# In-projection of a two-layer step: one ordered list of loads, two more tile buffers, and TensorE in written order

## Chip, cores, metric

One core of a Trainium2 chip. The metric is the device time of one execution in microseconds (us); the time of a kernel is the median of its runs.

## What is computed

One inference step of a two-layer backbone with D = 2048, for 128 context tokens and 128 latent tokens (256 columns in all). The change lies at the very start, in the first layer's modulated norm and its combined input projection:

```
mod = silu(cond) @ w_ada[0] + b_ada[0]                 # cond: two rows, (2, 2048) @ (2048, 6*2048)
sh1, sc1, gt1, sh2, sc2, gt2 = split(mod, 6)
h = rmsnorm(x, g_norm_mix[0]) * (1 + sc1) + sh1        # x: (256, 2048)
proj = h @ w_in_ab[0]                                  # (2048, 2880): queries, latents, keys, values
...                                                    # attention, out-projection, ConvFFN, second layer
```

Everything is float32. `w_ada[0]` is needed for sc1 and sh1 before any row of h exists; each is 2048 x 2048.

## The kernel before

Activations lie transposed: 16 chunks of 128 features on the partitions, 256 token columns (`x[:, c]`). A float32 product is made of three fast ones: each operand is split into a rounded high half and the rest (`hx` holds both halves of h; `wh`, `wl` those of a weight block), and `gemm` issues high x high, high x low, low x high for every 128 x 128 block. `split` does the halves: ScalarE casts the high one (L238), VectorE subtracts for the low one (L239). `Weights` loads tiles of 8 or 16 blocks into the buffers `raw` (three of 1 MB) and splits them when `chunk` runs out of blocks.

The in-projection (`mixer_ab`, `part`) runs over k in pieces, because h becomes ready piece by piece: chunks 0 and 1 against all 23 output columns, then chunks 2 and 3, then three times four chunks (quarters 2, 3 and 4). Each column's product goes to a PSUM tile `acc` (three of them) and is copied to (first piece) or added to (the others, VectorE, L957) the projection held in SBUF: `proj`, `kvb`, `qb`.

The adaLN vectors come from TensorE too: `condw` holds the two conditioning rows as a narrow stationary operand, and a *unit* (layer, vector j, quarter q) is four 1 MB tiles of `w_ada`, 16 matmuls in four column groups of one PSUM bank `ada` (`sum_rows`, L525 loads), a copy `am` to SBUF, four transposes, a reduction to `mod` and, for scales, one more step to `scl` (`ada_finish`). The first quarter of scale (j = 1) and shift (j = 0) is done in *half units* (`load_half`, `half_unit`, L358 and L368 to L378) of two tiles each, because only chunks 0 and 1 are needed to start. The adaLN tiles go to `araw` (two buffers); for the first eight units every second tile goes to one of the three `raw` buffers instead.

Before the first product the kernel loads all constants (`cst`), x in four pieces, the four tiles of two half units and a weight tile; takes the mean square of x (ScalarE squares, VectorE adds; `stat_rstd`, `norm_scale`); and makes the rows of chunks 0 and 1 with `modulate`: x times the norm factor (L597), scale and shift (L603 on VectorE, L606 on ScalarE), high half (L607), low half (L592, on VectorE and GpSimd by turns). Later rows are made by `modulate` once both units of their quarter are finished; `pump` and `ensure` spread the adaLN steps over the columns at set rates (`RATE`).

Order: a scheduler orders the instructions of each engine by a simulated time line, except for those passed to `keep_order`, which stay behind the instruction traced before them on their engine. `pe.in_turn` does this for all of TensorE's matmuls; before the change it is on in quarters 2 and 3 only. A load waits at the head of its queue (SP) until the buffer that it overwrites has been read.

Of the kernel before, what the change touches and what calls it, by code (L numbers as in the profile page):

```python
# [38 lines left out]
    ("ident", 128), ("ones", 128), ("pick", 32), ("inv", 5), ("mhalf", 16),  # L39
    ("rch", 128), ("rsh", 128), ("rcm", 128), ("rsm", 128),  # L40
    ("cond", 32), ("bada", NL * 6 * KD),
    ("gmix", NL * KD), ("gffn", NL * KD), ("gfin", 16),
# [8 lines left out]
NCONST = _n  # L51
RATE = {"in0": 0.35, "in": 0.5, "in3": 0.25, "heads": 0.72, "out0": 0.62, "c": 0.36, "outc": 0.36}
# [37 lines left out]
def step_kernel(ctx: ExitStack, tc: tile.TileContext, A: dict):  # L90
# [54 lines left out]
    sp.dma_start(out=cst, in_=A["cst"])  # L145
# [18 lines left out]
    act.activation(condw[:, :, 0:2], C("cond").rearrange("p (k r) -> p k r", r=2), AF.Silu)  # L164

# [49 lines left out]
    def bank():  # L215
        return T_(pmisc, [P, 512], "misc")
# [26 lines left out]
    class Weights:  # L243
# [9 lines left out]
        def load(self):  # L253
            raw = T_(wpool, [P, 4, 512], "raw").rearrange("p g n -> p (g n)")
            sp.dma_start(out=raw, in_=self.src[self.at])
            self.at += 1
            return raw

        def ahead(self, pin):

            if not self.half:
                self.half = [self.load(), 0]
            raw, lo = self.half
            self.blocks += self.halves(raw, lo, pin)
            self.half = None if lo else [raw, 8]

        def halves(self, raw, lo, pin=lambda i: i):
            wh = T_(wpool, [P, 1024], "wh", F32R, bufs=4)
            wl = T_(wpool, [P, 1024], "wl", F32R, bufs=4)
            for at in range(0, 8, FINE):  # L270
                s = slice(at * P, (at + FINE) * P)
                split(wh[:, s], wl[:, s], raw[:, (lo + at) * P:(lo + at + FINE) * P], pin)
            return [(wh[:, b * P:(b + 1) * P], wl[:, b * P:(b + 1) * P]) for b in range(8)]

        def chunk(self):
            while len(self.blocks) < self.nblk:
# [3 lines left out]
                n = self.per  # L280
                if self.cycle:
                    n = min(n, self.cycle - self.at * n % (-(-self.cycle // n) * n))
                n *= self.nblk if self.per < TB else 1
                raw = T_(wpool, [P, 4, 512], "raw").rearrange("p g n -> p (g n)")
                sp.dma_start(out=raw[:, :n * P], in_=self.src[self.at, :, :n * P])
                self.at += 1
                n0 = FINE if fine[0] else 8
                for lo in range(0, n, n0):
# [8 lines left out]
                    for b in range(hi - lo):  # L297
                        s = slice(b * P, (b + 1) * P)
                        self.blocks.append((wh[:, s], wl[:, s]))
            out, self.blocks = self.blocks[:self.nblk], self.blocks[self.nblk:]  # L300
            return out

    def first_three(W, xh, xl, order, mid=None, fixed=False):
# [3 lines left out]
        raws = [W.load() for _ in range(3)]  # L307
# [39 lines left out]
    ada = {"i": 2, "t": 0, "due": 0.0, "pew": 1.0}  # L347
# [6 lines left out]
    def load_half(j, h, tag):  # L354

        raws = [T_(wpool, [P, 4, 512], tag, **({"bufs": 2} if tag == "araw" else {})) for _ in range(2)]
        for t, raw in enumerate(raws):
            sp.dma_start(out=raw, in_=A["w_ada"][0, j, 0, 2 * h + t])  # L358
        return [raw.rearrange("p g n -> p (g n)").rearrange("p (b n) -> p b n", b=8) for raw in raws]

    def half_unit(j, h, raws, pin=lambda i: i):
        ps = T_(ppool["ada"], [P, 512], "ada", bufs=1)
        for k in range(KD):
            g = k % 4
            pin(pe.matmul(ps[32 * g:32 * g + 32, :NT], condw[:, k, :], raws[k // 8][:, k % 8],
                          start=(k < 4), stop=(k >= KD - 4), skip_group_check=True))
        am = T_(tmp, [P, 512], "am", bufs=1)
        act.copy(am[:, :NT], ps[:, :NT])  # L368
        pt = T_(ppool["ada"], [P, 512], "ada", bufs=1)
        for b in range(2):  # L370
            pe.transpose(pt[:, b * P:(b + 1) * P], am[:, b * P:(b + 1) * P], ident)
        at = slice(2 * h, 2 * h + 2)
        out = mod[:, 0, j, at]
        dve.tensor_reduce(out=out, in_=pt[:, :NT].rearrange("p (b g r) -> p b r g", b=2, g=4)[:, :, 0:2],
                          axis=AX.X, op=ALU.add)
        dve.tensor_tensor(out=out, in0=out, in1=vector("bada", 0, j, 0)[:, at], op=ALU.add)
        if j == 1:
            dve.scalar_tensor_tensor(out=scl[:, 0, 0, at], in0=out, scalar=1.0,  # L378
                                     in1=vector("gmix", 0, 0, 0)[:, at], op0=ALU.add, op1=ALU.mult)
        if h == 1:  # L380
            done.add((0, j, 0))
# [129 lines left out]

    def row_step(until=len(ROWS)):
# [68 lines left out]
    def norm_scale(st):  # L581
        return spread(stat_rstd(st, D))

    def modulate(hx, rb, l, which, chunks, fixed=False):
# [26 lines left out]
        for c, h in lows:  # L611
            low(c, h)

# [920 lines left out]
```

## Time and profile before

| | us |
|---|---|
| median of 3 runs | 2322.47 |
| lowest, highest | 2320.69, 2327.41 |
| profiled execution | 2323.0 |
| its span | 2321.2 |
| first product of the in-projection starts | 29.02 |
| first product on chunks 2 and 3 | 54.25 |
| quarter 2, quarter 3, quarter 4 start, about | 83, 128, 174 |

The profile shows one execution on the engines TensorE (PE, with its weight loads PEld), VectorE (DVE), ScalarE (ACT), GpSimd (POOL) and the load queue of SyncE (SP). Times in a row of the timeline are start and length; `xN` is a count; an arrow in brackets names what ended an idle stretch. A busy PE is not PE at its peak, since pipelined matmuls overlap in the records; start-to-start times are used for its rates.

### The profile page before, as it was taken

Reading aid. Unit: us, or ns where it says so; the run is one execution under the profiler, and the core shown is the slowest. Engines: PE = TensorE matmul, PEld = TensorE weight load, DVE = VectorE, ACT = ScalarE, POOL = GpSimd, SP = SyncE. Lnnn points to the kernel's source line nnn. Section 1 sums busy time; section 2 is a strip of 40 time slices with the busy share of each in tenths; the row PEclk is TensorE's granted clock in tenths of the full one; section 3 lists DMA queues with packets and bytes.
Section 4 is the critical chain, followed back from the end, with each engine's and each line's share of the span. In section 5 each row is a group of like instructions: output and inputs, shape, how many; then the busy total and the mean of one; then the engine's idle time right before and its main releaser. Section 6 shows DMA issues by size and latency. Waiting matters only on the chain.

```text
span 2321.2 us, 47505 instructions
## 1 busy us (share of the span) xinstructions
PE 2279.7 (98%) x19478; PEld 2183.0 (94%) x19478; DVE 1885.4 (81%) x2955; ACT 1202.8 (52%) x1982; POOL 197.7 (9%) x242
## 2 busy tenths in 40 slices
PE   6999999999999999999999999999999999999998
PEld 5778868999999999999999999999999999999998
DVE  4568978989999999999988979898999965666654
ACT  4246555575554355555575455457655434555543
POOL 0002211210000000000140001024000000000011
PEclk9999999999999999999999999999999999999999
DMA  9997888777777877777787888766767655555553
GB/s 373 338 345 271 327 312 307 288 287 262 261 265 280 307 266 255 260 266 258 281 323 279 299 324 303 294 258 221 255 251 272 254 200 200 191 191 199 192 192 127
DMA packets 99834, 617.15 MB, mean 266 GB/s; under 512 B 10720, under 2 KB 18720, under 8 KB 32928
## 3 DMA queue, kind: packets, MB, share of 16 engines
q1 hardware_dynamic: 99616, 614.11, 71.7%
q8 instruction: 153, 2.51, 0.4%
q14 instruction: 65, 0.53, 0.1%
HBM read 609.32 MB, written 4.75 MB: 265 GB/s over the span
## 4 chain that ended last, share of the span: by engine, by line
PE 83%; DMA 1%; DVE 0%; ACT 0%; POOL 0%; issue 0%; DVEq 0%; ACTq 0%
PE acc L105 80%; PE ada L105 1%; PE att L105 1%; DMA araw<-w_ada 1%; PE att L108 0%; DVE x L1396 0%; PE ada L108 0%; DVE wl L239 0%; PE misc L105 0%; ACT wh L238 0%; POOL rr L212 0%; DVE hx L239 0%; ACT hx L238 0%; ACT p L799 0%; PE misc L108 0%
## 5 line engine op out<-in xcount | busy, mean ns | idle before, releaser
L105 PE MATMUL acc<-hx,wh 128*128 128x256 f32 (+1 forms) x7264 | 1257.9, 278 | 4.4 <-ACT hx L607 1.4
L238 ACT CAST wh<-raw 128x1024 fp32r<-128x1024 f32 (+2 forms) x826 | 795.1, 974 | 881.2 <-PE acc L105 709.0
L105 PEld LDWEIGHTS acc<-hx,wh 128*128 128x128 f32 x7264 | 1098.8, 188 | 33.9 <-issue 14.7
L239 DVE TENSOR_TENSOR wl<-raw,wh 128x1024 fp32r<-128x1024 f32 (+2 forms) x826 | 923.0, 1133 | 247.8 <-ACT wh L238 242.9
L105 PE MATMUL acc<-hx,wl 128*128 128x256 f32 (+1 forms) x3632 | 1006.5, 278 | 5.3 <-DVE wl L239 5.3
L105 PEld LDWEIGHTS acc<-hx,wl 128*128 128x128 f32 x3632 | 683.7, 188 | 9.3 <-DVE wl L239 7.2
L105 PE MATMUL acc<-g,wh 128*128 128x256 f32 x2816 | 478.8, 276 | 0.0
L105 PEld LDWEIGHTS acc<-g,wh 128*128 128x128 f32 x2816 | 423.6, 188 | 0.0
L105 PE MATMUL acc<-g,wl 128*128 128x256 f32 x1408 | 388.0, 276 | 0.0
L433 DVE CUSTOM_DVE_ANT_0 junk<-araw,condb 128x2048 f32<-128x2048 f32 x128 | 294.2, 2298 | 0.0
L105 PE MATMUL acc<-hxc,wh 128*128 128x256 f32 (+1 forms) x1568 | 282.9, 282 | 0.0
L105 PEld LDWEIGHTS acc<-g,wl 128*128 128x128 f32 x1408 | 264.1, 188 | 0.0
L105 PEld LDWEIGHTS acc<-hxc,wh 128*128 128x128 f32 x1568 | 241.5, 189 | 4.6 <-issue 4.2
L105 PE MATMUL acc<-hxc,wl 128*128 128x256 f32 (+1 forms) x784 | 218.5, 279 | 0.0
L201 POOL TENSOR_TENSOR sqacc<-sqacc,sq 128x256 f32<-128x256 f32 x62 | 74.0, 1193 | 1499.3 <-ACT sq L197 1499.1
L105 PEld LDWEIGHTS acc<-hxc,wl 128*128 128x128 f32 x784 | 147.5, 188 | 0.4
L1288 ACT ACTIVATE cv<-acc,convw 128x256 f32<-128x256 f32 x169 | 94.4, 559 | 0.0
L105 PE MATMUL ada<-araw,condw 128*32 128x512 f32 (+1 forms) x640 | 78.6, 587 | 14.3 <-ACT sq L197 13.3
L485 DVE CUSTOM_DVE_ANT_0 hx<-block,condb 128x1024 fp32r<-128x1024 f32 x65 | 79.2, 1219 | 7.5 <-DMA block<-w_ada 5.4
L1294 DVE SCALAR_TENSOR_TENSOR cv<-acc,convw,cv 128x254 f32<-128x254 f32 x169 | 80.9, 479 | 3.2
L767 DVE SCALAR_TENSOR_TENSOR x<-acc,mod,x 128x128 f32<-128x128 f32 x190 | 57.2, 342 | 30.3 <-PE acc L105 30.3
L1291 DVE SCALAR_TENSOR_TENSOR cv<-acc,convw,cv 128x254 f32<-128x254 f32 x169 | 80.2, 475 | 0.0
(241 smaller groups left out, 1538.3 us busy)
## 6 DMA issues: line engine op xcount, KB each, us to landing
raw<-w_up SPq DMA_DIRECT2D x176, 1024.0 KB, 4.8
araw<-w_ada SPq DMA_DIRECT2D x138, 1024.0 KB, 5.7
raw<-w_down SPq DMA_DIRECT2D x88, 1024.0 KB, 4.8
raw<-w_in_c SPq DMA_DIRECT2D x48, 1024.0 KB, 6.5
block<-w_ada SPq DMA_DIRECT2D x41, 512.0 KB, 6.4
raw<-w_in_ab SPq DMA_DIRECT2D x19, 1024.0 KB, 7.2
raw<-w_out_ab SPq DMA_DIRECT2D x16, 1024.0 KB, 7.0
raw<-w_out_c SPq DMA_DIRECT2D x16, 1024.0 KB, 7.1
```

The lines of the kernel that those rows point to most:

```text
L105: return self.placed(nc.tensor.matmul(*a, **kw))
L201: eng.tensor_tensor(out=st["acc"], in0=st["acc"], in1=sq, op=ALU.add)
L238: pin(act.copy(out_hi, src))
L239: pin(dve.tensor_tensor(out=out_lo, in0=src, in1=out_hi.bitcast(F32), op=ALU.subtract))
L433: keep_order(dve.tensor_tensor_reduce(out=T_(feat["pool"], [P, D], "junk"), in1=feat["row"][:, c], in0=feat["raw"].rearrange("p g n -> p ( ...
L485: keep_order(dve.tensor_tensor_reduce(out=self.junk, in0=self.raw, in1=self.row[:, c].rearrange("p (g n) -> p g n", g=2), scale=1.0, scala ...
L767: dve.scalar_tensor_tensor(out=x[:, c, s], in0=ps[:, s], scalar=mod[:, l, 3 * which + 2, c, g:g + 1], in1=x[:, c, s], op0=ALU.mult, op1=AL ...
L1288: pin(act.activation(y, ps, AF.Identity, scale=cw[:, 1, m:m + 1], bias=cw[:, 3, m:m + 1]))
L1291: pin(dve.scalar_tensor_tensor(out=y3[:, :, 1:], in0=p3[:, :, :T - 1], scalar=cw[:, 0, m:m + 1], in1=y3[:, :, 1:], op0=ALU.mult, op1=ALU.add))
L1294: pin(dve.scalar_tensor_tensor(out=y3[:, :, :T - 1], in0=p3[:, :, 1:], scalar=cw[:, 2, m:m + 1], in1=y3[:, :, :T - 1], op0=ALU.mult, op1=A ...
```

## The change

Loads of the in-projection's first four pieces are put into one list, `feed`, in order of need: an entry is issued when a buffer of its kind is free, and an entry that has none holds all behind it. Buffers are counted by hand: three for weights, two `araw`, and two more of 1 MB, `s1` and `s3`, which lie where `ql` and `kv_in` will be later. Tiles 1 and 3 of a unit use these; weights have the three `raw` buffers to themselves.

TensorE's order is written out: `pe.in_turn` is on from the first half unit to the end of quarter 3, and dictionaries by column (`first_half`, `other_half`, `quarter`) say after which column a pair of adaLN tiles is summed (`pair`), a unit turned (`turned`) or rows begun. The matmuls of two tiles of a unit stand together.

The rows of chunks 0 to 7 are made in two steps: `scaled_rows` (norm factor and scale, before the shift is there) and `begin_row` (shift with the rounding to the high half on ScalarE, low half on VectorE). Quarters 3 and 4 still use `modulate`, now after column 19 instead of 18.

At the start: only the first 373 columns of constants are loaded ahead of x; the rest (`late_constants`) come in the list. The squares of x are taken in four pieces of four chunks. Nine idle matmuls on a zero tile (`WARM`) are issued first. The first weight tile is loaded in two halves, and its first half is split ahead of the first rows. The two half units no longer share a PSUM bank.

Quarter 4 and all later stages keep their code; the layout of the constants is reordered. The diff, cut:

```
+NEARLY = _AT["bada"][0] + 2 * KD
+WARM = 9
...
-    sp.dma_start(out=cst, in_=A["cst"])
+    keep_order(sp.dma_start(out=cst[:, :NEARLY], in_=A["cst"][:, :NEARLY]))
...
+            w = n * P // parts
+            for i in range(parts):
+                s = slice(i * w, (i + 1) * w)
+                pin(sp.dma_start(out=raw[:, s], in_=self.src[self.at, :, s]))
...
+    class Feed:
+        def __init__(self):
+            self.items, self.tiles = [], {}
+            self.free = {"a": 2, "s1": 1, "s3": 1, "raw": 3, "late": 1}
+        def add(self, home, load, key=None):
+            self.items.append((home, load, key))
+        def go(self):
+            while self.items and self.free[self.items[0][0]]:
+                home, load, key = self.items.pop(0)
+                self.free[home] -= 1
+                self.tiles[key] = load()
+        def use(self, home):
+            self.free[home] += 1
+            self.go()
...
-            if ada["i"] < 8 and t % 2:
-                ada["raw"] = T_(wpool, [P, 4, 512], "raw")
-            else:
-                ada["raw"] = T_(wpool, [P, 4, 512], "araw", bufs=2)
+            ada["raw"] = T_(wpool, [P, 4, 512], "araw", bufs=2)
...
+    def scaled_rows(rb, c0, n):
+        for c in range(c0, c0 + n):
+            h = T_(tmp, [P, NT], "nt", bufs=4)
+            keep_order(dve.tensor_tensor(out=h, in0=x[:, c], in1=rb, op=ALU.mult))
+            for g in range(2):
...
+                keep_order(dve.tensor_scalar(out=h[:, s], in0=h[:, s], scalar1=scl[:, 0, 0, c, g:g + 1],
+                                             scalar2=None, op0=ALU.mult))
...
+    def begin_row(hx, h, c):
+        for g in range(2):
...
+            keep_order(act.activation(hx[:, c, s], h[:, s], AF.Identity, bias=b_))
+            keep_order(dve.scalar_tensor_tensor(
+                out=hx[:, c, NT + g * T:NT + (g + 1) * T], in0=h[:, s], scalar=b_,
+                in1=hx[:, c, s].bitcast(F32), op0=ALU.add, op1=ALU.subtract))
...
+                half_load(1, 0)
+                half_load(0, 0)
+                weights(whole, 2)
+                half_load(1, 1)
+                weights(whole)
+                half_load(0, 1)
+                feed.add("late", late_constants)
+                weights(whole)
+                units(2, (0, 1))
+                weights(halves)
+                units(2, (2, 3))
+                weights(halves)
+                units(3, (0, 1, 2, 3))
+                weights(halves)
+                weights(rest)
+                for q in (1, 2):
+                    for u, ts in ((2 * q + 2, (0, 1)), (2 * q + 2, (2, 3)), (2 * q + 3, (0, 1)), (2 * q + 3, (2, 3))):
+                        weights(rest)
+                        units(u, ts)
+                    weights(rest)
+                    weights(rest)
+                feed.go()
+
+                pe.in_turn = True
...
+                whole.ahead(keep_order, first_rows)
...
+                first_half = {0: lambda: whole.ahead(keep_order), 4: lambda: half_begin(1), 6: lambda: half_end(1),
+                              10: lambda: stretch(2, 2), 13: lambda: half_begin(0), 15: lambda: half_end(0),
+                              22: lambda: pair(2, 0)}
+                other_half = {5: lambda: pair(2, 2), 7: turned, 10: lambda: stretch(4, 4), 12: lambda: pair(3, 0),
+                              15: lambda: pair(3, 2), 17: four_rows, 20: split_next, 22: split_next}
+                def quarter(q):
+                    u = 2 * q + 2
+                    return {4: lambda: pair(u, 0), 8: lambda: pair(u, 2), 10: turned, 13: lambda: pair(u + 1, 0),
+                            17: lambda: pair(u + 1, 2), 19: lambda: turned(q + 1)}
...
+                part(whole, 0, 2, True, 0, at(first_half))
+                part(halves, 2, 2, False, 0, at(other_half))
+                for q in (1, 2):
+                    part(rest, 4 * q, 4, False, 0, at(quarter(q)))
+                pe.in_turn = False
...
+        for _ in range(WARM):
+            keep_order(pe.matmul(ps, idle[:, :P], idle, start=True, stop=True))
```

More of the change, by code (lines that the diff above doesn't have):

```diff
@@ L164, in step_kernel @@
     act.activation(condw[:, :, 0:2], C("cond").rearrange("p (k r) -> p k r", r=2), AF.Silu)
+    warm = T_(small, [P, 2], "rv")
+    keep_order(act.activation(warm, condw[:, 0, 2:4], AF.Silu))
     def load_cw(l):
@@ L256, in load, with begin, take @@
             self.at += 1
-            return raw
-        def ahead(self, pin):
-            if not self.half:
[L262 to L267, printed above, removed]
+            return raw, n
+        def begin(self, parts=1):
+            self.begun.append(self.load(parts, keep_order))
+        def take(self):
+            return self.begun.pop(0) if self.begun else self.load()
@@ L268, in halves, with ahead @@
+        def ahead(self, pin, mid=None):
+            if not self.half:
+                self.half = [*self.take(), 0]
+            raw, n, lo = self.half
+            self.blocks += self.halves(raw, lo, pin, mid, min(8, n - lo))
+            self.half = None if lo else [raw, n, 8]
+            if lo:
+                self.used()
+        def halves(self, raw, lo, pin=lambda i: i, mid=None, n=8):
             wh = T_(wpool, [P, 1024], "wh", F32R, bufs=4)
             wl = T_(wpool, [P, 1024], "wl", F32R, bufs=4)
-            for at in range(0, 8, FINE):
-                s = slice(at * P, (at + FINE) * P)
-                split(wh[:, s], wl[:, s], raw[:, (lo + at) * P:(lo + at + FINE) * P], pin)
@@ L279, in chunk @@
                     continue
[L280 to L286, printed above, removed]
+                raw, n = self.take()
                 n0 = FINE if fine[0] else 8
@@ L352, in step_kernel @@
     later = []
[L354 to L381, printed above, removed]
```

235 lines of the change are left out of this document (175 added, 60 removed).

## The prediction

> **What bounds the kernel now.** I read the page first, then the busy time by stage, the waits of TensorE and of the load queue, and last the order of time. Bounds of the stages come from the timeline; columns are busy us (xcount) by engine, granted clock, DMA share, GB/s.
>
> ```profile
> span 2321.2 us, 47505 instructions
> PE 2279.7 (98%) x19478; PEld 2183.0 (94%) x19478; DVE 1885.4 (81%) x2955; ACT 1202.8 (52%) x1982; POOL 197.7 (9%) x242
> PE   6999999999999999999999999999999999999998
> ```
>
> ```profile
> 0.00:29.00 29.00, 12.33 (x96) 6.30 (x96) 10.71 (x31) 11.67 (x28) 1.41 (x6) 1.00 0.95 385
> 29.00:54.25 25.25, 24.54 (x207) 20.04 (x207) 10.75 (x21) 15.16 (x36) 1.96 (x2) 0.93 0.92 352
> 54.25:83.08 28.83, 25.82 (x198) 19.89 (x195) 18.02 (x43) 9.40 (x16) 2.02 (x2) 0.94 0.97 375
> 83.08:127.80 44.72, 43.21 (x349) 34.60 (x349) 26.17 (x50) 15.30 (x22) 1.63 (x2) 1.00 0.89 325
> 127.80:174.00 46.20, 43.46 (x353) 34.92 (x352) 26.82 (x50) 15.43 (x23) 1.45 (x2) 1.00 0.90 344
> ```
>
> TensorE is busy in every slice but the first, so a microsecond taken from its path in the in-projection should reach the end. The five rows are: before the first product; part A (chunks 0 and 1, with the first pair of adaLN tiles of the second quarter's shift-and-scale units); part B (chunks 2 and 3); quarter 2; quarter 3. Quarter 4 starts at about 174. No engine but TensorE is near its full time in any row, and the DMA is below its best rate in the last four.
>
> ```profile
> 126.78 0.39 PE L105 MATMUL acc<-hx,wh 128*128 128x256 f32 x2
> 127.12 0.39 PE L105 MATMUL acc<-hx,wh 128*128 128x256 f32 x2
> 86.03 1.07 PE L105 MATMUL ada<-araw,condw 128*32 128x512 f32 x8
> 87.02 0.50 PE L105 MATMUL acc<-hx,wh 128*128 128x256 f32 x2
> 26.57 1.07 PE L105 MATMUL ada<-araw,condw 128*32 128x256 f32 x16 [0.27 <-DVE mod L374]
> 101.29 0.60 PE L108 MATMUL ada<-cst,am 128*128 128x128 f32 x4
> ```
>
> These are TensorE's prices. Three products take 0.34 us from start to start (126.78 to 127.12): 0.1133 each. A 1 MB adaLN tile takes 0.99 (86.03 to 87.02), so a unit of four 4.0; a tile of the first quarter takes 1.07, a half unit of two 2.1; turning a unit takes about 0.5 of the quoted 0.60. Work of the stages at these prices: part A 138 products = 15.6, two half units 4.3, their turns 0.8, two tiles 2.0: 22.7 of 25.25. Part B 15.6, six tiles 5.9, two turns 1.0: 22.5 of 28.83. Quarters 2 and 3 each 276 products = 31.3, two units 8.0, two turns 1.0: 40.3 of 44.72 and 46.20. So 2.5, 6.3, 4.4 and 5.9 us lie between work, and 29 us before it.
>
> ```profile
> 13.34 1.94 PE L105 MATMUL ada<-araw,condw 128*32 128x256 f32 x16 [13.34 <-ACT sq L197]
> 21.68 3.64 PE L105 MATMUL ada<-raw,condw 128*32 128x256 f32 x32 [1.17 <-DVE mod L374]
> 29.02 1.60 PE L105 MATMUL acc<-hx,wh 128*128 128x256 f32 x4 [1.37 <-ACT hx L607]
> 28.00:32.00 4.00, 2.98 (x12) 2.68 (x13) 2.82 (x6) 1.27 (x4) 1.22 (x1) 0.62 1.00 411
> 72.00:76.00 4.00, 2.19 (x18) 1.19 (x10) 1.91 (x7) 3.31 (x6) 0.00 (x0) 1.00 0.95 320
> 76.00:80.00 4.00, 3.25 (x15) 3.25 (x16) 3.89 (x8) 3.61 (x8) 2.02 (x2) 0.59 1.02 401
> 108.23 0.50 PE L105 MATMUL acc<-hx,wh 128*128 128x256 f32 x2
> 109.49 0.39 PE L105 MATMUL acc<-hx,wl 128*128 128x256 f32 x1 [0.76 <-DVE wl L239]
> 173.59 0.74 PE L105 MATMUL acc<-hx,wh 128*128 128x256 f32 x4 [0.86 <-ACT wh L238]
> ```
>
> ```profile
> SPq L525 <- PE ada L105: 42.5, 19, 4.0
> ```
>
> Three kinds of loss are visible. The shift's half unit starts only at 21.68, since both half units share one PSUM bank, and it runs at half clock (32 in 3.64, against 16 in 1.07). The second quarter's rows wait for their unit in part B: TensorE is half idle at 72 to 76 and then gets a clock of 0.59. In the quarters a product waits for the low half of a weight tile that landed late (109.49, 173.59), because the load queue had waited for buffers: in the first 230 us it waited 42.5 for adaLN sums alone.
>
> **The change, part by part.**
>
> ```profile
> 8.00:12.00 4.00, 0.00 (x0) 0.00 (x0) 3.09 (x8) 2.99 (x8) 0.00 (x0) 1.00 1.04 430
> 16.00:20.00 4.00, 4.00 (x27) 2.71 (x27) 0.16 (x1) 0.37 (x1) 0.70 (x1) 1.00 1.02 426
> cst<-cst SPq DMA_DIRECT2D x1, 698.5 KB, 4.0
> x<-xT SPq DMA_DIRECT2D x4, 512.0 KB, 7.0
> araw<-w_ada SPq DMA_DIRECT2D x24, 1024.0 KB, 7.3
> 8.26 0.72 ACT L197 ACTIVATE sq<-x 128x256 f32<-128x256 f32 x2 [0.38 <-DMA x<-xT]
> ```
>
> *Landing times.* The queue runs at about 424 GB/s while nothing blocks it. The constants and the first adaLN tile are 3.86 MB, 9.1 us at this rate, and are used at 13.34; constants and two pieces of x are 1.76 MB, 4.2 us, used at 8.26. So a tile lands about 4.1 us after the list's bytes over 0.424. The new list starts with 373 of the constants' columns (0.19 MB), x 2.10, and four tiles 4.19: 6.48 MB, landed at 19.4; the first half of the first weight tile follows at 20.6.
>
> ```profile
> 25.44 0.37 ACT L368 COPY am<-ada 128x256 f32<-128x256 f32 x1 [6.07 <-PE ada L105]
> 27.79 0.88 ACT L606 ACTIVATE nt<-nt,mod,scl 128x128 f32<-128x128 f32 x2
> L239 DVE TENSOR_TENSOR wl<-raw,wh 128x1024 fp32r<-128x1024 f32 x31 | 37.2, 1220 | 15.2 <-ACT wh L238 15.1
> L238 ACT CAST wh<-raw 128x1024 fp32r<-128x1024 f32 x32 | 32.2, 1050 | 57.1 <-DMA raw<-w_in_ab 51.5 <-DVE proj L957 5.6
> L957 DVE TENSOR_TENSOR proj<-proj,acc 128x256 f32<-128x256 f32 x33 | 13.6, 419 | 27.2 <-PE acc L105 27.2
> L603 DVE TENSOR_SCALAR nt<-nt,scl,mod 128x128 f32<-128x128 f32 x16 | 4.5, 342 | 0.1
> L105 PE MATMUL misc<-cst,rr 128*128 128x128 f32 x4 | 1.2, 462 | 0.0
> ```
>
> *The front.* Last tile 19.4, its sums 1.07 to 20.5; ScalarE first casts the weight half (pinned ahead, landed 20.6, about 0.55) and then copies the sums, 0.4, to 21.6; two transposes and two small VectorE steps bring the shift by 22.8; one row's two activations 0.9 more. First product at about 24.0 instead of 29.0: 5.0 gained. The nine idle products (nine of two passes) are unpriced: four passes over 128 columns took 1.2, so 512 columns are about 1 us a pass cold, half of that warm; 9 to 18 us from about 1. Below 12 they are hidden, since the first tile lands at 12.0; above, they delay only the scale's half unit, which has until 19.4. I take no cost; at the far bound the first product is some 3 us later.
>
> The clock: in the row 28 to 32 it fell to 0.62 although no idle stretch just before exceeded 1.37. TensorE will again be mostly idle from 20.5 to 24, so I charge the same half-clock stretch once more, 1.7 us. [...]
>
> *Part A*: 22.7 of work, 1.7 of clock, 0.6 of small gaps: 24.0 to 49.0, against 54.25. Gain so far 5.2. Its second and third weight tiles land at 29.3 and 37.7; with 2.3 for cast and low half (the rows of L238 and L239) they are there at 31.6 and 40.0, when TensorE wants them at about 33 and 41. It fits without slack.
>
> *Part B*: the rows of the second quarter are scaled early (moved, so nothing new), and at their shift only an activation and one VectorE step per half remain; the stall at 72 to 76 and its slow clock go. Next late is the third weight tile: 26.7 MB into the list, landed 67.0, usable 69.3, needed at about 67; and VectorE has 23 adds of 0.419, 5.75 low halves of 1.22, two tiles split ahead for 2.4, four rows of about 1.1 and six of 0.7: 27 us of work in a stretch of 25, some of it started earlier. I charge 2.0. Part B ends at 49.0 + 22.5 + 2.0 = 73.5 against 83.08: gain 9.5.
>
> *Quarters 2 and 3*: with four adaLN buffers and three for weights a load no longer waits for the tile just before it. In quarter 3 a pair of buffers comes free at the fifth column; the next pair lands some 7.3 (the araw row) and 2.5 later and is used 15 us on, after nine columns of 1.36, another pair and a turn. I leave 1.5 of small gaps to each: 41.8 and 41.8, against 44.72 and 46.20: 7.3 gained, of which I keep 6.5, for the rows of the next quarter now have three columns (4 us) of cover instead of four; that cover gone, they would cost about 2.
>
> *Quarter 4 and after* keep their rates and start 16 earlier, at 158. The scheduler may order a few things otherwise; I take 0.5 off. Sum: 9.5 + 6.5 - 0.5 = 15.5 less than the profiled execution's 2323.0 (its span of 2321.2 and 1.8 around it), which is 0.5 above the median of 2322.47: 2307.
>
> **Rivals.** *The load rate* (0.15). Over a longer stretch the trace shows 375 GB/s (54 to 83), with blocked loads in it. Were that the rate itself, part B's last weight tile is usable at 77.6 and quarter 2 starts at about 83, as now; only 6.5 remain: 2316. [...]
>
> *Slower: the written order* (0.13). Before, in parts A and B, TensorE could take any ready product; now it stands at a pair of adaLN tiles until both have landed, and all weights wait behind. Twelve pairs stand there. Each late pair costs its lateness, and above some 1.4 us of idle also a slow clock, 1.7. The gain is gone at 1.3 us a pair; at 2 us it is 24 lost against 15.5 won: 2331. For it: no slack in part A, one blocked entry holds all loads behind it, and ScalarE's copy of the sums is pinned too, so that casts queue behind a late pair. Against it: from part B on, by the landing times above, pairs are early.
>
> *It does not reach the end* (0.05): a later stage bound by loads would give the time back: 2320. The page's slices after the first speak against it.
>
> **How the numbers follow.** 0.3%, about 7 us, is what a measurement here can tell from no change. The forecast has 0.67, with 9 to 23 of gain (3 from the idle products, 2 from VectorE and rows, 2 from order on the one side; the clock, the charged gaps on the other). Faster 0.67, within 0.3% 0.20 (load rate and lost gain), slower 0.13. The range reaches from 2299 over the first two rivals to 2322.
>
> **What would show it.** First product at 23 to 25 and part B's start near 49: front right. A granted clock under 0.7 after it: the clock step right. Quarter 2 starting at 72 to 76 with rates above 410 until 60: the list right; at 82 or later with the share at 1.0: the load rate. Waits of TensorE for adaLN tiles, or idle gaps ahead of pairs, totalling over 10: the written order. Quarters of 41 to 43 confirm the buffers. Wrong would be a first product after 27, or quarter 4 starting after 168.

## The result, and the profile after

| | us |
|---|---|
| before, median of 6 runs | 2325.07 (2320.69 to 2327.41) |
| changed, median of 6 runs | 2309.88 (2308.48 to 2311.19) |
| changed / before | 0.9937, 95% interval 0.9925 to 0.995 |
| changed, profiled execution and its span | 2308.48, 2306.7 |

The change makes the kernel 0.6% faster: 14.5 us between the two profiled spans, where the prediction's sum was 15.5, and both 2309.88 and 2308.48 lie within its range. The medians above differ by 15.2; in a later group of runs, where the kernel before had 2320.56, the same changed kernel was 11.7 below it, so the gain is known to a few us only. The page of the changed kernel looks as before; only the first slice has moved.

```profile
span 2306.7 us, 47528 instructions
PE   8999999999999999999999999999999999999998
```

The busy time by stage says where the gain came from. Columns as in the prediction's table; the rows are the stretch before the first product, part A, part B, quarters 2, 3 and 4, and the heads up to the first residual of the out-projection. First the changed kernel, then two rows of the kernel before, quarter 4 and the heads, which the prediction did not show.

```profile
0.00:24.30 24.30, 18.07 (x106) 8.80 (x106) 7.76 (x18) 7.82 (x13) 1.41 (x6) 0.99 0.92 355
24.30:50.90 26.60, 25.89 (x222) 21.86 (x222) 11.36 (x28) 16.98 (x40) 0.00 (x0) 0.88 0.95 390
50.90:78.50 27.60, 23.78 (x197) 18.39 (x194) 19.29 (x49) 7.96 (x16) 0.00 (x0) 1.00 1.01 414
78.50:121.40 42.90, 41.11 (x333) 34.45 (x332) 27.64 (x55) 16.33 (x22) 0.00 (x0) 0.96 0.91 367
121.40:162.80 41.40, 41.40 (x353) 35.05 (x352) 27.31 (x52) 16.83 (x25) 1.64 (x2) 1.00 0.89 350
162.80:210.00 47.20, 47.20 (x392) 42.08 (x391) 38.45 (x84) 31.00 (x65) 11.90 (x13) 1.00 0.71 265
210.00:355.80 145.80, 141.57 (x1010) 114.57 (x1012) 117.20 (x287) 78.02 (x182) 25.19 (x48) 1.00 0.85 317
```

```profile
173.80:219.90 46.10, 45.86 (x374) 40.87 (x374) 37.82 (x80) 30.14 (x61) 10.61 (x11) 1.00 0.72 260
219.90:368.90 149.00, 144.06 (x1010) 115.00 (x1013) 117.11 (x287) 78.30 (x182) 28.81 (x48) 0.99 0.83 310
```

| stage | before | predicted | measured | gain so far, predicted | measured |
|---|---|---|---|---|---|
| front | 29.0 | 24.0 | 24.3 | 5.0 | 4.7 |
| part A | 25.2 | 25.0 | 26.6 | 5.2 | 3.3 |
| part B | 28.8 | 24.5 | 27.6 | 9.5 | 4.6 |
| quarters 2 and 3 | 90.7 | 83.6 | 84.3 | 16.0 | 11.0 |
| quarter 4 | 46.1 | | 47.2 | | 9.9 |
| heads | 149.0 | | 145.8 | | 13.1 |
| all the rest | | | | 15.5 | 14.5 |

Parts A and B together gained nothing (54.2 us after, 54.1 before) where 4.5 were forecast; the heads, whose code was not touched, became 3.2 shorter. Quarter 4 of the kernel before is taken to start at 173.8, with its row above. The bound of quarter 2's start (78.5) is counted from the turn of the second quarter's shift (74.74): five columns of 0.68 and the turn.

**Front.** TensorE's timeline (start, length), then two rows of the busy time:

```profile
20.49 1.07 PE L107 MATMUL att<-kv_in,condw 128*32 128x256 f32 x16 [1.42 <-DMA kv_in<-w_ada]
22.70 0.44 PE L110 MATMUL att<-cst,am 128*128 128x128 f32 x2 [1.14 <-ACT am L390]
24.32 0.97 PE L107 MATMUL acc<-hx,wh 128*128 128x256 f32 x2 [1.19 <-ACT hx L672]
```

```profile
24.00:28.00 4.00, 3.68 (x16) 3.58 (x17) 2.81 (x7) 3.04 (x8) 0.00 (x0) 0.50 1.02 424
28.00:32.00 4.00, 4.00 (x36) 3.52 (x38) 0.40 (x1) 1.61 (x4) 0.00 (x0) 0.66 1.01 420
```

The last shift tile's sums start at 20.49, 1.1 later than the 19.4 that was counted for its landing, and the chain of copy, turn and activation behind them takes 3.8 to the first product at 24.32, where 4.6 was counted: the chain is the one that was counted, and its two errors nearly cancel. The clock then falls to 0.50 and 0.66; the longest idle stretch since 12 is the one of 1.42.

**Part B.** Here TensorE waits for weight halves. Its waits from 50.9 to 78.5 (us in total, times, longest), its timeline around the longest, and the timeline of ScalarE:

```profile
PE acc L107 <- DVE wl L246: 2.1, 3, 1.0
PE acc L107 <- ACT wh L245: 1.7, 1, 1.7
```

```profile
72.22 0.50 PE L107 MATMUL acc<-hx,wh 128*128 128x256 f32 x2 [1.71 <-ACT wh L245]
73.48 0.39 PE L107 MATMUL acc<-hx,wl 128*128 128x256 f32 x1 [0.76 <-DVE wl L246]
...
81.07 0.38 PE L107 MATMUL acc<-hx,wl 128*128 128x256 f32 x1 [1.49 <-DVE wl L246]
```

```profile
57.91 0.59 ACT L424 COPY am<-ada 128x512 f32<-128x512 f32 x1 [6.48 <-PE ada L107]
58.39 2.00 ACT L245 CAST wh<-raw 128x1024 fp32r<-128x1024 f32 x2
70.64 0.59 ACT L424 COPY am<-ada 128x512 f32<-128x512 f32 x1 [10.25 <-PE ada L107]
71.12 1.78 ACT L245 CAST wh<-raw 128x1024 fp32r<-128x1024 f32 x2
```

ScalarE stands idle for 10.25 us in front of the copy of a unit's sums, and the casts of the next weights go right behind it. This copy (L424) is not among the instructions passed to `keep_order`; the scheduler put it there. Until TensorE comes to that pair ScalarE splits no weight, and TensorE then runs out of split ones. The weight tiles were there by then: the trace has the second one of part B landed at 55.9 and the third at 68.9, and their casts start at 58.4 and 71.1, each at the end of a copy. Then VectorE is full (3.75 and 4.00 of 4), and the clock falls again, to 0.74:

```profile
76.00:80.00 4.00, 3.28 (x27) 2.90 (x25) 3.75 (x13) 4.00 (x12) 0.00 (x0) 1.00 0.99 367
80.00:84.00 4.00, 2.93 (x17) 2.93 (x18) 4.00 (x10) 2.23 (x3) 0.00 (x0) 0.74 1.02 432
```

```profile
77.96 0.41 DVE L639 TENSOR_TENSOR nt<-x,misc 128x256 f32<-128x256 f32 x1
```

The last row is one of four multiplies of the *next* quarter's rows, which the scheduler put among the low halves that quarter 2 waits for.

**Loads.** The list kept the queue going: from 44 to 76 every stretch of 4 us has 412 to 428 GB/s. The one hole in parts A and B is at 40 to 44, after 406 at 36 to 40.

```profile
40.00:44.00 4.00, 3.47 (x44) 2.51 (x36) 1.12 (x1) 2.48 (x5) 0.00 (x0) 1.00 0.65 221
```

What the buffers did shows at ScalarE, in its waits from 78 to 216 (us in total, times, longest) for weight tiles to land. Before, in the changed kernel, and in the two runs below that go without the two extra buffers (e3, f4):

```profile
ACT wh L238 <- DMA raw<-w_in_ab: 52.0, 9, 11.2
ACT wh L245 <- DMA raw<-w_in_ab: 9.1, 3, 3.8
ACT wh L245 <- DMA raw<-w_in_ab: 41.8, 8, 10.1
ACT wh L245 <- DMA raw<-w_in_ab: 37.7, 7, 6.8
```

### The profile page after: what moved, and what is told of

Same layout as the page of the kernel before. It is cut to its first block, busy times and chain, and to the rows that moved or that the text cites. A ratio compares the mean times of both kernels' runs of the same rounds, so it can differ in the third digit from the quotient of the medians.

```text
span 2306.7 us, 47528 instructions
## 1 busy us (share of the span) xinstructions
PE 2278.7 (99%) x19504; PEld 2186.1 (95%) x19504; DVE 1887.0 (82%) x2967; ACT 1202.5 (52%) x1973; POOL 188.5 (8%) x238
## 4 chain that ended last, share of the span: by engine, by line
PE 84%; DMA 0%; DVE 0%; ACT 0%; POOL 0%; issue 0%; DVEq 0%; ACTq 0%
PE acc L107 81%; PE ada L107 1%; PE att L107 1%; PE att L110 0%; DMA araw<-w_ada 0%; DVE x L1589 0%; PE ada L110 0%; PE misc L107 0%; DVE wl L246 0%; ACT wh L245 0%; POOL rr L219 0%; DVE hx L246 0%; ACT hx L245 0%; ACT p L862 0%; PE misc L110 0%
## 5 line engine op out<-in xcount | busy, mean ns | idle before, releaser
L107 PE MATMUL ada<-araw,condw 128*32 128x512 f32 (+1 forms) x608 | 73.8, 578 | 1.3 <-DMA araw<-w_ada 1.3
```

The lines of the kernel that those rows point to most:

```text
L107: return self.placed(nc.tensor.matmul(*a, **kw))
```

## The experiments

All were timed in five rounds beside the kernel before. Landmarks compare profiled executions: the first pair of adaLN sums in quarter 2 (changed kernel 89.47), the first in quarter 3 (130.53), and the first copy of the heads (209.97, before 219.91).

| kernel | median us | ratio to before (95%) | quarter 2 pair | quarter 3 pair | heads |
|---|---|---|---|---|---|
| changed, again (a0_again) | 2308.84 | 0.9943 (0.993 to 0.9955) | 88.73 | 129.65 | 209.09 |
| e1_no_idle | 2312.91 | 0.9959 (0.9946 to 0.9971) | 92.18 | 133.46 | 212.77 |
| e2_free_order | 2313.69 | 0.9966 (0.9954 to 0.9979) | 90.63 | 135.09 | 216.70 |
| e3_no_extra_buffers | 2317.17 | 0.9979 (0.9971 to 0.9988) | 89.79 | 135.02 | 217.74 |
| e4_rows_late | 2311.32 | 0.9954 (0.994 to 0.9967) | 89.60 | 130.90 | 212.00 |
| e5_weights_first | 2310.54 | 0.9952 (0.9939 to 0.9964) | 89.61 | 130.52 | 211.24 |
| e6_cast_ahead | 2308.71 | 0.9943 (0.9931 to 0.9955) | 87.98 | 129.08 | 210.55 |
| e7_keep_clock | 2312.00 | 0.9956 (0.9942 to 0.997) | 93.25 | 134.27 | 213.71 |
| f1_multiply_later | 2310.47 | 0.9941 (0.9927 to 0.9955) | 88.26 | 130.88 | 212.27 |
| f2_cast_and_multiply | 2308.09 | 0.9932 (0.9919 to 0.9944) | 86.02 | 128.64 | 210.03 |
| f3_free_order_multiply | 2312.38 | 0.995 (0.9938 to 0.9963) | 88.93 | 132.46 | 212.86 |
| f4_no_buffers_multiply | 2318.45 | 0.9982 (0.9972 to 0.9991) | 87.68 | 131.31 | 215.35 |

The medians of the kernel before in the three groups were 2321.31 (e1 to e4), 2320.56 (a0, e5 to e7) and 2322.85 (f1 to f4). Two executions of the changed kernel differ by 0.7 to 0.9 at these landmarks, so less than 1 us tells nothing there; where a landmark is said to be so much later, the two figures compare with these two executions.

### First group: one part undone at a time

**No idle products.**

```
-WARM = 9
+WARM = 0
```

> The changed kernel without the nine idle products at the start. My theory: the first sums run at half clock again (16 in about 1.9 us instead of 1.07) and the first product comes 1 to 2 us later than 24.3; parts A and B are then held by landed tiles, so little of it reaches the end: 13 to 15 us under the kernel before, where the changed kernel is 15.2 under. Rival (the idle products keep the clock up, and the front's gain is theirs): part A starts 3 to 4 us later and the gain falls to about 11 us.

The first product moves from 24.3 to 26.7 and the delay stays, 2.8 to 3.7 at the heads; by the medians 3.0 to 4.1 are lost. So it is not hidden behind landed tiles, as I had expected (8.4 under the kernel before, not 13 to 15). TensorE's timeline shows why, first of this kernel, then of the changed one:

```profile
13.37 1.94 PE L107 MATMUL ada<-araw,condw 128*32 128x256 f32 x16 [13.37 <-DMA araw<-w_ada]
15.23 3.57 PE L107 MATMUL misc<-cst,kvb 128*128 128x1 f32 x16
...
22.18 1.51 PE L107 MATMUL att<-ql,condw 128*32 128x256 f32 x16
23.52 1.04 PE L107 MATMUL att<-kv_in,condw 128*32 128x256 f32 x16
```

```profile
7.62 4.46 PE L107 MATMUL acc<-am 128*128 128x512 f32 x10
13.11 1.07 PE L107 MATMUL ada<-araw,condw 128*32 128x256 f32 x16 [1.04 <-DMA araw<-w_ada]
14.11 1.95 PE L107 MATMUL misc<-cst,kvb 128*128 128x1 f32 x16
```

Sixteen sums take 1.94 instead of 1.07 and the statistics 3.57 instead of 1.95. The idle products fill the time from 7.62 (and before) to 12.1, ahead of the first tile at 13.1; without them TensorE runs at half rate from its first work to about 23, though the granted clock of these stretches reads 1.00, as in this row of e1. The idle products earn 3 to 4 us.

```profile
16.00:20.00 4.00, 4.00 (x26) 3.32 (x29) 0.16 (x1) 0.00 (x0) 0.70 (x1) 1.00 1.00 416
```

**TensorE's order left to the scheduler in the front and in parts A and B.**

```
-                pe.in_turn = True
...
+                pe.in_turn = True
```

> The changed kernel with TensorE's written order only in quarters 2 and 3, as before; in parts A and B the scheduler may place products and adaLN sums. My theory: the order itself gives nothing, the loads and buffers do; within 2 us of the changed kernel, so 13 to 17 us under the kernel before. Rival (the written order is the gain): 6 us or more are lost, so at most 9 under.

Quarter 2's pair comes 1.2 to 1.9 later, but the larger loss is at the start of quarter 3, where a row's low half is late and the clock falls behind it:

```profile
127.26 0.39 PE L107 MATMUL acc<-hx,wh 128*128 128x256 f32 x1 [1.72 <-DVE hx L634]
```

```profile
128.00:132.00 4.00, 4.00 (x25) 4.00 (x24) 1.75 (x4) 1.05 (x1) 0.00 (x0) 0.63 0.72 303
```

By the medians the written order is worth some 4 us, where I had expected 2 at most (this kernel's profiled execution, 2316.55, lay 2.9 above its median, so its landmarks overstate the loss); whether all of it is TensorE's order is asked again below (f3).

**No extra tile buffers**: tiles 1 and 3 take weight buffers, as before the change.

```
-                    home = ("a", "s1", "a", "s3")[t]
+                    home = ("a", "raw", "a", "raw")[t]
```

> The changed kernel without the two extra buffers: tiles 1 and 3 of a unit take one of the three weight buffers, as before; list and written order stay. My theory: the load queue waits for buffers again, part B and the quarters lose most of what they won: 5 to 8 us worse than the changed kernel, 7 to 10 under the kernel before. Rival (the list's order alone is enough): under 2 us worse, 13 or more under.

The largest single loss, 7 to 8 us by the medians, but not where I looked for it: up to quarter 2's pair it is as the changed kernel to within 1.1 us. The loss begins at quarter 3's rows (135.02 against 130.53), with waits of 0.81 and 1.45 for their high and low halves at 124 to 126, and it grows to 7.8 by the heads. Tiles land late again: ScalarE waits 41.8 us for them, as shown above. From quarter 2's pair to the heads TensorE has no wait of over 0.6 for a half of a weight tile, though; it waits for rows and adds.

**Second quarter's rows begun late**: their shift is not written with the turn.

```
-                    turned()
-                    for i, h in enumerate(second["nt"]):
-                        begin_row(hx, h, 4 + i)
+                    turned(1)
...
-                other_half = {5: lambda: pair(2, 2), 7: turned, 10: lambda: stretch(4, 4), 12: lambda: pair(3, 0),
+                other_half = {5: lambda: pair(2, 2), 7: turned, 12: lambda: pair(3, 0),
```

> The changed kernel with the second quarter's four rows made whole after their unit is turned (by modulate, at the same column), not scaled ahead. My theory: VectorE is full from 76 to 88 us in the changed kernel and moving four multiplies and eight scalings into that stretch costs 2 to 4 us: 11 to 13 under the kernel before. Rival (late weight tiles hold TensorE there, not the rows): under 1 us worse, 14 to 15 under.

Quarters 2 and 3 start as in the changed kernel to within 1.3 us, and the median is 1.4 to 2.5 us higher, with intervals that overlap. Scaling the rows ahead of their shift, one part of the change, brings 2.5 us at most, and nothing clear at quarter 2's own start.

Taken against the kernel before of their own group, the four parts undone cost 3.3, 4.1, 7.6 and 1.7 us of the 11.7 that the changed kernel has in a0: together more than the whole gain, so their worths cannot be added up. No run undoes the list itself, the divided loads at the start or the separate bank for the second half unit.

### Second group: what holds part B

**The changed kernel again**, with no edit.

> The changed kernel itself, unedited, beside the next three on the same chip, so that they can be compared with it. All theories: 14 to 16 us under the kernel before.

Its median repeats the time to 1 us; that it is only 11.7 under the kernel before, and not 14 to 16, is for the most part that kernel's median, 4.5 lower than in the first group. The place of the slow clock does not repeat. After the same idle gaps (1.12 and 1.19 instead of 1.14 and 1.19) it reads 1.00 from 24 on, and it had fallen earlier, at 16 to 20, where the first execution has 1.00:

```profile
16.00:20.00 4.00, 4.00 (x36) 2.24 (x39) 0.75 (x5) 0.37 (x1) 0.70 (x1) 0.57 1.01 420
24.00:28.00 4.00, 3.58 (x26) 3.22 (x27) 3.07 (x7) 3.41 (x10) 0.00 (x0) 1.00 1.03 424
```

There it costs nearly nothing: the sums take 1.65 and 1.34 instead of 1.07, but the last tile's start at 20.59 instead of 20.49, since the first execution stood 1.42 for that tile. By the end of part A the repeat is only 0.9 us ahead (first pair there at 48.15, against 49.05).

**Weights ahead of adaLN tiles in the list.**

```
-                units(2, (0, 1))
+                units(2, (0,))
                 weights(halves)
-                units(2, (2, 3))
+                units(2, (1, 2, 3))
```

> The changed kernel with one entry of the list moved: the first weight tile of part B stands ahead of the second quarter's tile that waits for the s1 buffer, so that the 4 us hole in the transfers at 40 to 44 closes. Theory A (part B waits for landed tiles): the weight tiles of part B come 2 us earlier, the waits at 50.9, 59.8, 69.5 and 72.2 and the slow clock after 80 shrink, 2 to 4 us better than the changed kernel. Theory B (part B's casts stand behind ScalarE's copy of the adaLN sums, tiles have landed): under 1 us either way.

The hole in the transfers closes (221 GB/s became 397; a smaller one opens at 52 to 56, with 317), and TensorE's waits for low halves stay at 4.3 us:

```profile
40.00:44.00 4.00, 3.39 (x44) 2.43 (x34) 1.16 (x2) 2.52 (x5) 0.00 (x0) 1.00 0.99 397
```

Quarters 2 and 3 start as in the changed kernel, and the median is 1.7 above that of a0, with overlapping intervals. So the landing of these tiles does not bound part B, and the theory that it does falls.

**Casts of the next weights written ahead of each pair's copy.**

```
+                def cast_then(w, step):
+                    def both():
+                        w.ahead(keep_order)
+                        step()
+                    return both
...
-                              22: lambda: pair(2, 0)}
+                              22: cast_then(halves, lambda: pair(2, 0))}
-                other_half = {5: lambda: pair(2, 2), 7: turned, 10: lambda: stretch(4, 4), 12: lambda: pair(3, 0),
+                other_half = {5: cast_then(halves, lambda: pair(2, 2)), 7: turned, 10: lambda: stretch(4, 4), 12: lambda: pair(3, 0),
```

(and likewise at columns 13 and 15.)

> The changed kernel with four half tiles of weights cast and split ahead of a pair of adaLN sums (columns 13 and 22 of part A, 5 and 15 of part B), so that ScalarE does them before it stands at the copy of the sums. Theory B (casts behind that copy): TensorE's waits for weight halves at 43.0, 50.9, 59.8, 69.5 and 72.2 (4.5 us) mostly go, and the slow clock after 80 with them: 3 to 5 us better than the changed kernel. Theory A (tiles land late): under 1 us better, perhaps worse, since ScalarE then stands at the load.

TensorE's waits from 24.3 to 165, the main ones:

```profile
PE acc L107 <- DVE proj L1126: 1.7, 1, 1.7
PE acc L107 <- ACT wh L245: 1.3, 1, 1.3
...
PE acc L107 <- DVE wl L246: 0.9, 2, 0.6
```

The waits for low halves shrink from 4.3 (five) to 0.9 (two). But ScalarE's timeline shows that in part B the order which the edit was to change is as it was:

```profile
57.18 0.59 ACT L424 COPY am<-ada 128x512 f32<-128x512 f32 x1 [5.78 <-PE ada L107]
57.67 2.18 ACT L245 CAST wh<-raw 128x512 fp32r<-128x512 f32 x4
69.75 0.59 ACT L424 COPY am<-ada 128x512 f32<-128x512 f32 x1 [9.90 <-PE ada L107]
70.23 4.21 ACT L245 CAST wh<-raw 128x512 fp32r<-128x512 f32 x8
```

The copy isn't pinned, and it still comes first, with much the same idle time in front (6.48 and 10.25 in the changed kernel). The tiles of these casts landed at 57.5 and 69.6 in this run, so there was little to win by going ahead. What differs is the size: `ahead` splits in pieces of 512 elements where the changed kernel's casts have 1024, and a low half is ready sooner; the wait for the cast itself only goes from 1.7 to 1.3. Only in part A does a cast stand ahead of a copy (41.1 and 42.3), the pinned one of a half unit, and there the wait of 0.69 for a low half is gone. So this run prices smaller pieces in the main, and not the copy's place. A new wait of 1.7 stands at 83, for an add on VectorE, which is now the engine that is full:

```profile
80.00:84.00 4.00, 3.34 (x26) 3.10 (x26) 4.00 (x7) 1.06 (x1) 0.00 (x0) 1.00 1.01 422
```

Quarter 2 comes 0.7 to 1.5 earlier, the end does not move; 3 to 5 us had been expected.

**Three more idle products between the half units' steps.**

```
+                def idle_product():
+                    pe.matmul(T_(pacc, [P, 512], "acc"), ident, x[:, 0:2].rearrange("p c n -> p (c n)"),
+                              start=True, stop=True)
...
                 unit.copy()
+                    idle_product()
                 unit.turn()
```

> The changed kernel with three more idle products, one after each sum of the first shift unit and one after its turn, in the idle stretches at 19 to 24. If idle stretches of 1.2 to 1.4 us in a row are what lowers the clock at 24 to 30: it stays at 1.0, the first part's first pair of tiles is summed 2 to 3 us earlier than 49.05, and 1 to 3 us reach the end. [...]

The products (1.12 for the one at 22.46, two records in the trace) stand in the way: the first product starts at 27.05, every landmark is 3.7 to 4.6 late, and by the medians 2.1 to 3.2 us are lost, where a gain of 1 to 3 had been expected if gaps of 1.2 to 1.4 lower the clock. The clock is 1.00 from 24 to 32, but it was 0.50 at 16 to 20 and 0.72 at 20 to 24, ahead of or among these products. Runs e3, e5 and f4, which have the changed kernel's idle products and no others, likewise show 0.50 at 16 to 20 and 1.00 from 24 on. So this run does not show that the idle products held the clock; it shows that they cost more than the 0.9 by which the two executions of the changed kernel differ.

### Third group: VectorE's share

**The next rows' multiplies pinned at column 12 of the quarter before**, in all four. In f1 alone:

```
     def modulate(hx, rb, l, which, chunks, fixed=False, begun=None):
...
-            pin(dve.tensor_tensor(out=h, in0=x[:, c], in1=rb, op=ALU.mult))
+            h = begun.pop(0)
...
-                    return {4: lambda: pair(u, 0), 8: lambda: pair(u, 2), 10: turned, 13: lambda: pair(u + 1, 0),
+                    return {4: lambda: pair(u, 0), 8: lambda: pair(u, 2), 10: turned, 12: lambda: multiplies(q + 1), 13: lambda: pair(u + 1, 0),
```

> The changed kernel with the four multiplies by the norm factor that begin the rows of quarters 3 and 4 pinned behind column 12 of the quarter before; in the changed kernel the scheduler puts those of quarter 3 on VectorE at 78 to 83 us, where VectorE is full, and those of quarter 4 at 123 to 125. Theory C (VectorE bounds the stretch from 76 to 88): 1.65 us leave it, quarter 2's first pair of tiles is summed 1 to 2 us earlier after its turn, 1 to 3 us better than the changed kernel. Rival (late weight tiles bound it): within 1 us.

Quarter 2 comes 0.5 to 1.2 earlier, and 1.28 are lost at 123 on a row's low half; nothing of the expected 1 to 3 us is left at the end.

**Both: casts ahead (e6) and multiplies later (f1).**

> The casts pinned ahead of the pairs and the multiplies pinned later, both. Theory C: once VectorE is relieved, the waits that the earlier casts remove are no longer handed on to quarter 2's start: 2 to 4 us better than the changed kernel, 16 to 18 under the kernel before. Rival: within 1 us of the changed kernel, as the earlier casts alone were.

Together they move quarter 2 more than either alone: its pair at 86.02, 2.7 to 3.5 earlier. (In part B the copies stand ahead of the casts here too, at 56.36 and 68.98, so that what e6's edit changes there is again the size of the pieces.) It is handed back at the next boundaries, beginning with 1.28 at 121 on a row's low half, and the heads start at 210.03, no earlier than in the changed kernel. At 2308.09 it has the lowest median of all, but it lies 0.8 and 1.8 us from the changed kernel's two medians, and the intervals overlap: not shown to be faster, where 2 to 4 us were expected.

**e2's free order with f1's multiplies.**

> Parts A and B without TensorE's written order, with the multiplies pinned later. If most of what the free order lost (5 to 6 us) came from VectorE's order around quarter 3's rows (TensorE stood 1.7 us at 125 for a low half and then ran at a clock of 0.63), it is 1 to 3 us behind the kernel with the multiplies alone, and that stall is gone. If the loss is TensorE's own order in parts A and B: still 5 or more behind.

Of the delay of 4.6 to 5.4 at quarter 3 in e2, 1.6 remain against f1 (132.46 and 130.88). But the wait itself, which I had expected gone, is still there, with 1.45 at 124 for a row's low half. The clock stayed at 1.00 behind it this time (three products still take 0.34, 125.91 to 126.25). The free order in parts A and B costs 1.9 us by the medians (2312.38 and 2310.47, with overlapping intervals); that the rest of e2's loss was order on VectorE and the fall of the clock fits this, and is not shown by it.

**e3's buffers with f1's multiplies.**

> Without the two extra buffers, with the multiplies pinned later. If the buffers' worth (8 us in the earlier run) is load waits: still 6 or more behind the kernel with the multiplies alone. If about half of it was the same stall of VectorE's order at quarter 3's rows: 3 to 5 behind, and the stall at 123 to 127 is gone.

Quarters 2 and 3 come as in f1 to within 0.6, so the missing buffers cost TensorE 1 us at most up to there, although ScalarE waits 37.7 us for tiles (2.0 in f1). Yet the median is 8.0 above f1's. Of the 5.2 between the two profiled executions (2316.93 and 2311.73), 3.1 arise by the heads, where quarter 4's rows hold VectorE:

```profile
164.00:168.00 4.00, 2.29 (x16) 1.76 (x15) 4.00 (x6) 1.36 (x5) 3.05 (x2) 1.00 1.02 424
168.00:172.00 4.00, 3.85 (x21) 3.79 (x21) 0.49 (x2) 1.99 (x2) 0.00 (x0) 0.60 1.02 420
```

and 2.5 in the heads (0.4 come back later), which take 149.1 (215.35 to 364.45). The heads of the kernel before take 149.0, those of every other kernel here 145.8 to 146.8. Both kernels with 149 have one wait of 2.0 that none of the others has. Before:

```profile
296.08 0.30 PE L108 MATMUL att<-cst,p 128*128 128x128 f32 x1 [2.05 <-DVE p L824]
```

and in f4 the same wait, of 2.01, at 291.78. But TensorE waits for `p` at other places too, and all its waits for it in the heads of the kernel before and of the changed one are

```profile
PE att L108 <- DVE p L824: 3.4, 3, 2.0
PE att L110 <- DVE p L887: 2.7, 2, 1.4
```

and 4.5 in f4. So this wait goes with the 149, and it accounts for 0.7 to 1.8 of the 3.2 us; for the rest no run gives a cause.

## Why the prediction was right, and where it was not

*The front* was right in its chain: 24.3 for 24.0, with the last tile 1.1 later and the chain behind it 0.8 shorter than counted. The idle products hid as assumed, and e1 prices what the sum used without naming it: the sums took 1.07 for sixteen with idle products ahead of them and 1.94 without, and without them 3 to 4 us are lost.

*The clock step* (1.7 once more) was right in kind, but its place and size were luck. By an estimate from the rows 24 to 32 the clock took some 3.2 us (half of 3.68, a third of 4.00); in the repeat it fell at 16 to 20 and took next to nothing from part A, and the end of part A differs by 0.9. Which idle stretch lowers the clock is not shown: 0.50 and 0.66 came behind gaps of at most 1.42, while 1.00 was read from 72 to 80, behind one of 1.71. The fast side of the prediction's range counts on a clock that does not fall. No run with the idle products at the start shows that: each of the twelve executions has 4 us at 0.50 to 0.64 between 12 and 32.

*Part A* was 1.6 too short: that clock and a wait of 0.69 at 43 for a low half. *Part B* is the step that failed. I charged 2.0 for VectorE and the last weight tile; its waits for weight halves are 3.8, and at quarter 2's start follow 0.3, 1.49 and a clock of 0.74. "Next late is the third weight tile" named the wrong thing. That tile landed at 68.9, 1.9 later than counted, and would have been late for a TensorE that came at 67; but TensorE came for it at 70.5, and ScalarE in all of part B waited for no tile, only 16.7 us for the two units' sums and 2.9 for the shift. Late was the split: the casts stood behind the copies (read from the order and the landing times; no edit moved them), pieces of 1024 made the low halves later still (e6, where pieces of 512 took the waits for low halves from 4.3 to 0.9), and at quarter 2's start low halves stood behind adds and the next quarter's multiplies (f1). My count of VectorE, 27 us of work in 25 (its terms add up to 27.7), was the right warning, but I spread it over the stretch, while the four rows, the next quarter's multiplies and the low halves all fall between 76 and 88.

*Quarters 2 and 3* came to 84.3 for 83.6, and 6.4 of gain where 6.5 was taken. I gave it to the loads. For the loads that is right: ScalarE's wait for weight tiles fell from 52.0 to 9.1 and rises to 41.8 and 37.7 without the two buffers. How it reaches TensorE is not what I described. I had products waiting for halves of late tiles; without the buffers (f4) these quarters run as fast to within 1 us, and the buffers' 8 us come in at rows and adds of quarters 3 and 4 and later, on a full VectorE (3.97 of 4 at 124 to 128 in e3, 4.00 at 164 to 168 in f4). That late tiles push the splits together with the rows is a likely link, and no run tests it.

*Quarter 4 and after* were charged 0.5 and gave 3.5: a loss of 1.1, a gain of 3.2 in the heads, and 1.4 in the rest. The code is the same; the scheduler may have found another order, and the wait of 2.0 for `p` goes with the longer heads, in the kernel before and in f4. It is less than the 3.2, and why the heads differ was not tested.

*The rivals.* Load rate: fell. Rates of 412 to 428 held from 44 to 76 us, where 375 was its premise. Written order: fell. From 24.3 to 165 TensorE waits for no adaLN tile at all (4.3 for low halves, 1.7 for a cast, 1.2 for a row and 0.3 for an add), where the rival had twelve late pairs, and the order as a whole gains 2 to 4 (e2, f3). Its side remark, casts that queue behind ScalarE's copy, is what part B shows, though the prediction was wrong to call that copy pinned: only those of the half units are. Not reaching the end: fell, with 11.0 at quarter 4's start and 14.5 at the end. The signs named beforehand hold for the front (24.3), the low clock, quarters of 42.9 and 41.4, and quarter 4 at 163, ahead of 168; the rates hold but for 406 and 221 at 36 to 44, quarter 2 at 78.5 lies outside 72 to 76, and part B's start at 50.9 is late of 49.

So the total was right partly by offset: 5 too much for parts A and B, 4 too little for what comes later.

## What to carry to other kernels

When a kernel's loads are put in order and its tensor engine's order is written out, look next at the engine that splits the operands: here a copy of 0.59 that waited for the tensor engine held back the casts queued behind it, and the profile shows it as an idle stretch of 10.25 on that engine ahead of the copy. After an edit of the order, look in the trace whether the order has changed; here it had not, and the shorter waits for low halves (0.9 instead of 4.3) came from smaller pieces. Add up an engine's work for the few microseconds around a boundary and not for the whole stage, and look for a stall removed ahead of one boundary at the next, as here 1.28 at 121 for a row's low half, with VectorE busy 3.82 of 4 from 120 to 124 (f2). With a scheduler that orders the rest, a stage whose code is untouched, the heads, moved by 3.2 us; take an edit of a few microseconds to be worth that much less or more until the total is measured.

## What was unexpected of the hardware

TensorE's rate at the start is not seen in the granted clock: without idle products sixteen sums took 1.94 instead of 1.07 at a granted 1.00 (e1, 12 to 16). And where the granted clock falls after partly idle stretches differed between two executions of one kernel. The twelve executions with the idle products at the start (the changed kernel twice, and all runs but e1) each have a stretch of 4 us between 12 and 32 with a clock of 0.50 to 0.64; in four of them (the changed kernel's first, e4, e6, f3) the clock falls only at about 24, in the others before. The changed kernel had 0.50 and 0.66 at 24 to 32 in one execution and 0.57 at 16 to 20 in the other, with gaps of 1.14 and 1.19, and of 1.12 and 1.19, between 21 and 24 (and one of 1.42 at 19.1 to 20.5 in the first alone), and fell in both at 80 to 84 (0.74 and 0.66), where TensorE's longest idle stretch was 1.49 in the one and it was busy for 3.82 of 4 in the other. What sets the place, no run here shows.
